# First layer's modulation as columns out of TensorE, and the context's h in two vector passes

## The chip, the cores and the metric

The kernel runs on one core of one Trainium2 chip. The metric is the device time of one execution in microseconds (us). The core has five engines that run side by side, each with its own program: TensorE (PE, with its weight loads shown apart as PEld), VectorE (DVE), ScalarE (ACT), GpSimd (POOL) and SyncE (SP, which issues most DMAs). Each engine works through its program in order and waits on semaphores of the others.

## The reference

Two transformer blocks of two layers each follow one another, all in float32 on 512 latent tokens of 1024 features; the first block has 256 context tokens too. The change touches only what stands ahead of the first layer's projection:

```python
mod = c_silu @ ada_w + ada_b             # (1, 3072): shift, scale, gate
mod_c = cctx_silu @ ada_w + ada_b        # the same weights, the context's vector
shift, scale, gate = jnp.split(mod, 3, axis=-1)
shift_c, scale_c, gate_c = jnp.split(mod_c, 3, axis=-1)
hx = rmsnorm(x, norm_w) * (1 + scale[:, None, :]) + shift[:, None, :]
hc = rmsnorm(cx, norm_w) * (1 + scale_c) + shift_c
px = split_cols(hx @ w_in)
pc = split_cols(hc @ w_in)
```

## The kernel before

Activations lie transposed: features on the 128 partitions (8 tiles `k`), tokens along the free dimension. A float32 product of large matrices is made of three products in `mm3` (L289 to L291): each operand is split into a high part and a low remainder, and hi·hi, hi·lo and lo·hi are summed. For weights ACT makes the high part (`whi<-wraw`, L203) and DVE the remainder (`wlo`, L204); `Weights` does that one tile ahead of its use.

`start` is the stage in question. SP loads x (four DMAs), the vectors, and 16 tiles `aw` of 512 KB: the shift and scale columns of the first layer's modulation weights, cut into four chunks of 512 columns, in the order `ADA0`. `ada0` makes one chunk in 8 matmuls of full float32 (L409): the two condition vectors (`ccol`, 128x2) are the stationary operand, 512 weight columns stream past, and 2 rows of 512 results appear. ACT copies the rows out of PSUM (L412), four transposes on PE turn them into columns (`adac`, L415), and DVE copies these (L416). `mods` (L430, L434) adds the bias and makes the scale columns `acol`. One float32 matmul stands in the trace as two records, a load and a matmul each.

Between them stand the norm of x (squares on ACT, sums on DVE, four matmuls against ones at L249, a power on POOL at L259, four transposes `rrow` at L266 that spread it over the partitions, and eight multiplications of x in place at L583), and the same for the context `cx`, whose loads come last. `h` makes hx in two halves of four tiles, then hc: ACT writes the high part (L589), DVE the full value `hmod` (L590) and the remainder (L591). The first half of hx needs the first two chunks, the second half all four. The first projection tile (`dps<-hx,whi`, L289) follows: 8 tiles k times three matmuls.

A tile framework decides the order of the instructions on each engine when the program is built; the order differs from the code's, and is fixed from then on.

Of the kernel before, what the change touches and what calls it, by code (L numbers as in the profile page):

```python
# [9 lines left out]
F32 = mybir.dt.float32  # L10
# [3 lines left out]
AF = mybir.ActivationFunctionType  # L14
OP = mybir.AluOpType
# [4 lines left out]
D = 1024  # L20
KD = 8
N = 512
NC = 256
# [47 lines left out]
def fr(ap):  # L71
    return ap.bitcast(F32)


class Weights:
# [139 lines left out]
    def next(self, n=None):  # L215
        at = self.n_use
        if self.extra is None:
            self.cut(at + (n or self.depth))
        else:

            self.cut(at + min(n or 2, 2))
            with self.tc.issue_after(self.K.mm_last):
                self.cut(at + (n or self.depth))
                while self.sums and self.sums[0][0] <= at:
                    _, f, m, kc = self.sums.pop(0)
                    f(m, kc)
        self.load(len(self.loads))
        return self.ready.pop(0)[1:]
# [48 lines left out]
def drain(g):  # L277
    for _ in g:
        pass


class Kern:
# [4 lines left out]
    def mm3(self, ps, hi, lo, xh, xl, start, stop):  # L287
        mm = self.nc.tensor.matmul
        mm(ps, hi, xh, start=start, stop=False)  # L289
        mm(ps, hi, xl, start=False, stop=False)  # L290
        self.mm_last = mm(ps, lo, xh, start=False, stop=stop).ins  # L291
        return self.mm_last
# [103 lines left out]
    def ada0(self, part, aw):  # L396


        nc, a, c = self.nc, self.a, self.cst
        if part == 0:  # L400
            self.mod0 = self.adap.tile([128, 24, 2], F32, tag="mod0", bufs=1, name="mod0")
        for ch in ADA0[2 * part:2 * part + 2]:
            ps = self.pt("d", "adaps")
            for g in range(4):
                next(aw, None)
                t = self.aw.pop(0)
                for kk in range(2):
                    k = 2 * g + kk
                    nc.tensor.matmul(ps[0:2, :], self.cc[:, k, :], t[:, kk, :], start=k == 0, stop=k == 7)  # L409
                yield  # L410
            row = self.adap.tile([128, D], F32, tag="adaw", name="adarow")[0:2, :512]
            nc.scalar.activation(row, ps[0:2, :], AF.Copy)  # L412
            pc = self.pt("pt", "adac")
            for t in range(4):
                nc.tensor.transpose(pc[:, 2 * t:2 * t + 2], row[:, t * 128:(t + 1) * 128], self.ident[0:2, 0:2])  # L415
            nc.vector.tensor_copy(self.mod0[:, 4 * ch:4 * ch + 4, :], pc[:, :8].rearrange("p (t s) -> p t s", s=2))  # L416
            yield

    def mods(self, l, cols=((0, 24),)):
# [140 lines left out]
    def start(self, s):  # L560

        nc, a = self.nc, self.a
        V, A = nc.vector, nc.scalar
        self.tmp = s.enter_context(self.tc.tile_pool(name="tmp0", bufs=3))
        xp = s.enter_context(self.tc.tile_pool(name="xp0", bufs=1))
        x = xp.tile([128, 8, N], F32, name="x")
        cx = xp.tile([128, 8, NC], F32, name="cx")
        aw = self.ada0_load(xp)
        for k in range(0, 8, 2):
            nc.sync.dma_start(x[:, k:k + 2, :], a["xt"][:, k:k + 2, :])  # L570
            if k:
                next(aw)
        for _ in range(9):
            next(aw)

        def norm(t, n):
            acc = xp.tile([128, 512], F32, tag="acc", bufs=2, name="acc")
            for k in range(8):
                self.sq_acc(acc[:, :n], t[:, k, :], k)
            nm = Norm(self)  # L580
            nm.part([acc], 0, n)
            for k in range(8):
                V.tensor_tensor(t[:, k, :], t[:, k, :], nm.R[:, :n], op=OP.mult)  # L583

        def h(t, n, hs, s_, k0):
            for k in range(k0, k0 + 4):
                sc, sh = self.A[0][:, k, s_:s_ + 1], self.mod[0][:, k, s_:s_ + 1]
                m = self.tmp.tile([128, 512], F32, tag="hmod", name="hmod")
                A.activation(hs[0][:, k, :], t[:, k, :], AF.Identity, bias=sh, scale=sc)  # L589
                V.tensor_scalar(m[:, :n], t[:, k, :], sc, sh, op0=OP.mult, op1=OP.add)  # L590
                V.tensor_tensor(hs[1][:, k, :], m[:, :n], fr(hs[0][:, k, :]), op=OP.subtract)  # L591

        norm(x, N)
        for i in range(2):
            drain(self.ada0(i, aw))
            self.mods(0, [(4 * i, 4 * i + 4), (8 + 4 * i, 12 + 4 * i)])
            if i:
                with self.tc.issue_after(self.last_load.ins):
                    self.W.load(1)
                    for k in range(0, 8, 4):  # L600
                        nc.sync.dma_start(cx[:, k:k + 4, :], a["ctxt"][:, k:k + 4, :])
                    self.W.load(3)
            h(x, N, self.hx, 0, 4 * i)
        norm(cx, NC)
        for i in range(2):
            h(cx, NC, self.hc, 1, 4 * i)

    def useg(self, i, k, o):

# [742 lines left out]
class Block2:  # L1352
# [155 lines left out]
    def seven(self, pool, banks):  # L1508
# [7 lines left out]
        def product(ps, b, start):  # L1516
            hi, lo = K.W.next()
            for k in range(4):
                mm(ps, hi[:, k, :], b[0][:, k, :], start=k == 0 and start, stop=False, skip_group_check=True)  # L1519
                mm(ps, hi[:, k, :], b[1][:, k, :], start=False, stop=False, skip_group_check=True)  # L1520
                K.mm_last = mm(ps, lo[:, k, :], b[0][:, k, :], start=False, stop=k == 3, skip_group_check=True).ins  # L1521
                self.step()
# [892 lines left out]
```

## Time and profile before

| | |
|---|---|
| median of 3 runs | 2479.59 us (2479.31 to 2483.43) |
| the profiled execution | 2483.87 us |
| its span, first to last instruction | 2482.1 us |
| PE busy | 2354.0 us (95%), 14392 matmul records |
| DVE busy | 1902.7 us (77%) |
| ACT busy | 1326.0 us (53%) |
| mean granted TensorE clock | 0.983 |

The span is the time from the first to the last instruction on the core; what is left of the execution's own time, 1.8 us, lies around it. The granted clock is TensorE's: 1.00 is 2.4 GHz and 0.50 is 1.2 GHz.

### The profile page before, as it was taken

What the parts mean: (1) busy time and instruction counts of PE and PEld (TensorE: products, weight loads), DVE (VectorE), ACT (ScalarE), POOL (GpSimd) and SP (SyncE); (2) the same over time, 40 slices, a digit from 0 to 9 for tenths busy, and PEclk for the clock granted to TensorE, in tenths of its full rate; (3) what the DMA queues carried; (4) which work ended last, traced back from release to release, by engine and by line L of the source; (5) the groups of instructions that cost most, each with busy time, mean ns of one, the idle gap of its engine ahead of it and who ended that gap; (6) DMA issues with size and microseconds to landing.
All of it is one profiled execution on the core that took longest, in us unless ns stands there. A gap on an engine that the chain in (4) does not pass through costs nothing. (4 is left out here: it accounts for less than half of the span.)

```text
span 2482.1 us, 37640 instructions
## 1 busy us (share of the span) xinstructions
PE 2354.0 (95%) x14392; PEld 2028.6 (82%) x14392; DVE 1902.7 (77%) x3337; ACT 1326.0 (53%) x2595; POOL 113.0 (5%) x138
## 2 busy tenths in 40 slices
PE   7899999999999999999998899999999799999998
PEld 3788888888887788888786678989898578899997
DVE  5778777888457888798669868989767985967674
ACT  3566555667345665568644455535354455545453
POOL 0100000000011100000010101000001010100000
PEclk9999999999999999999999999999999999999999
DMA  6112333223422136641432122675432212242422
GB/s 257 51 50 92 96 105 100 85 88 100 153 81 76 45 124 204 211 131 50 135 99 67 58 63 86 215 242 208 141 102 74 69 57 68 85 137 69 136 65 72
DMA packets 87749, 269.67 MB, mean 109 GB/s; under 512 B 12049, under 2 KB 22545, under 8 KB 87185
## 3 DMA queue, kind: packets, MB, share of 16 engines
q1 hardware_dynamic: 78240, 232.79, 29.1%
q10 hardware_dynamic: 6912, 25.17, 2.9%
q0 software_dynamic: 2416, 9.31, 1.0%
q8 instruction: 113, 1.85, 0.3%
q14 instruction: 68, 0.55, 0.1%
HBM read 255.82 MB, written 11.40 MB: 108 GB/s over the span
## 5 line engine op out<-in xcount | busy, mean ns | idle before, releaser
L289 PE MATMUL dps<-hx,whi 128*128 128x512 f32 (+1 forms) x1040 | 412.7, 398 | 22.1 <-ACT q L1744 8.1
L291 PE MATMUL dps<-hx,wlo 128*128 128x512 f32 (+1 forms) x1040 | 400.1, 386 | 8.3 <-DVE wlo L204 4.3
L290 PE MATMUL dps<-hx,whi 128*128 128x512 f32 (+1 forms) x1040 | 401.0, 387 | 5.7 <-DVE hx L523 4.4
L203 ACT ACTIVATE whi<-wraw 128x1024 fp32r<-128x1024 f32 (+2 forms) x202 | 194.1, 964 | 272.6 <-issue 93.6
L204 DVE TENSOR_TENSOR wlo<-wraw,whi 128x1024 fp32r<-128x1024 f32 (+1 forms) x182 | 209.3, 1151 | 75.9 <-ACT whi L203 74.5
L289 PEld LDWEIGHTS dps<-hx,whi 128*128 128x128 f32 x1040 | 200.9, 193 | 51.3 <-ACT q L1744 8.9
L291 PEld LDWEIGHTS dps<-hx,wlo 128*128 128x128 f32 x1040 | 200.2, 193 | 44.5 <-DVE wlo L204 5.2
L290 PEld LDWEIGHTS dps<-hx,whi 128*128 128x128 f32 x1040 | 200.5, 193 | 31.5 <-DVE hx L523 7.1
L1162 ACT ACTIVATE ph<-PT 128x512 fp32r<-128x512 f32 (+1 forms) x280 | 152.8, 559 | 136.1 <-PE PT L1157 132.8
L1163 DVE TENSOR_TENSOR pl<-PT,ph 128x512 fp32r<-128x512 f32 (+1 forms) x280 | 175.2, 641 | 43.4 <-ACT ph L1162 41.2
L161 ACT ACTIVATE whi<-wraw 128x512 fp32r<-128x512 f32 x200 | 118.7, 625 | 102.5 <-PE spt L1520 38.4
L1145 PE MATMUL Y<-ph,vt 128*128 128x256 f32 (+1 forms) x592 | 161.8, 283 | 6.7 <-ACT ph L1162 2.8
L1157 PE MATMUL PT<-ident,P 128*128 128x128 f32 x1024 | 160.5, 276 | 5.8 <-DVE pl L1163 4.0
L1146 PE MATMUL Y<-pl,vt 128*128 128x256 f32 (+1 forms) x592 | 163.1, 291 | 2.4 <-DVE pl L1163 2.2
L290 PE MATMUL w2p<-g,whi 128*128 128x512 f32 (+1 forms) x364 | 140.9, 387 | 1.0 <-DVE g L299 1.0
L289 PE MATMUL w2p<-g,whi 128*128 128x512 f32 (+1 forms) x364 | 140.8, 387 | 0.0
L291 PE MATMUL w2p<-g,wlo 128*128 128x512 f32 (+1 forms) x364 | 140.6, 387 | 0.0
L1157 PEld LDWEIGHTS PT<-ident,P 128*128 128x128 f32 x1024 | 119.0, 141 | 23.1 <-DVE pl L1163 9.8
L1145 PEld LDWEIGHTS Y<-ph,vt 128*128 128x128 f32 x592 | 112.2, 190 | 28.5 <-ACT ph L1162 19.5
L1096 PE MATMUL S<-kt,qt 128*128 128x256 f32 (+2 forms) x576 | 127.3, 329 | 1.6 <-DVE nm L1114 0.9
L1146 PEld LDWEIGHTS Y<-pl,vt 128*128 128x128 f32 x592 | 112.3, 190 | 13.5 <-DVE pl L1163 6.0
L1115 ACT ACTIVATE P<-P,nm 128x512 f32<-128x512 f32 (+1 forms) x128 | 94.9, 742 | 47.7 <-DVE nm L1114 46.1
(474 smaller groups left out, 6387.6 us busy)
## 6 DMA issues: line engine op xcount, KB each, us to landing
wraw<-ffn_w SPq DMA_DIRECT2D x120, 512.0 KB, 4.4
wraw<-w_in SPq DMA_DIRECT2D x112, 512.0 KB, 3.5
adaw<-ada_wt SPq DMA_DIRECT2D x80, 512.0 KB, 4.0
adab<-ada_wt ACTq DMA_DIRECT2D x48, 512.0 KB, 5.1
wraw<-w_out SPq DMA_DIRECT2D x32, 384.0 KB, 3.1
aw<-ada_w SPq DMA_DIRECT2D x16, 512.0 KB, 10.2
wraw<-w_out SPq DMA_DIRECT2D x16, 512.0 KB, 3.5
bias<-bias_b SPq DMA_DIRECT2D x16, 384.0 KB, 3.7
```

Of the source, the lines that this page charges most:

```text
L161: self.nc.scalar.activation(hi[:, j * w:j * w + w], x, AF.Copy)
L203: s = self.nc.scalar.activation(hi[:, q], t[:, q], AF.Copy)
L204: v = E.tensor_tensor(lo[:, q], t[:, q], fr(hi[:, q]), op=OP.subtract)
L289: mm(ps, hi, xh, start=start, stop=False)
L290: mm(ps, hi, xl, start=False, stop=False)
L291: self.mm_last = mm(ps, lo, xh, start=False, stop=stop).ins
L1096: mm(S[:, so:so + n], Q[:, j, qc], Kt[:, i, ko:ko + n], start=i == 0, stop=i == 1)
L1145: mm(o, v, ph[:, co:co + w], start=b == 0 and n == 0, stop=False, skip_group_check=True)
L1146: mm(o, v, pl[:, co:co + w], start=False, stop=b == len(banks) - 1 and n == len(items) - 1, skip_group_check=True)
L1157: nc.tensor.transpose(pst[:, col:col + 128], ps[t][:, pc:pc + 128], K.ident)
L1162: A.activation(ph[:, :col], pst[:, :col], AF.Copy)
L1163: V.tensor_tensor(pl[:, :col], pst[:, :col], fr(ph[:, :col]), op=OP.subtract)
```

## The change

`ada0` swaps the operands. A 128x128 piece of the weights is now the stationary operand and `ccol`, two columns wide, streams past it, so that the results come out as columns; 32 matmuls make a chunk in place of 8, and ACT's copy and the four transposes are gone. For the context, the three passes of DVE (times R in place, scale and shift, remainder) become two: cx times scale times R into `hmod`, then shift and remainder in one. ACT writes hc's high part from `hmod`, so it now comes after DVE's first pass. Line numbers behind the first part of the diff fall by 3 up to `start`, and rise by 3 behind it.

```diff
             for g in range(4):
                 next(aw, None)
-                t = self.aw.pop(0)
+                w = self.aw.pop(0)
                 for kk in range(2):
                     k = 2 * g + kk
-                    nc.tensor.matmul(ps[0:2, :], self.cc[:, k, :], t[:, kk, :], start=k == 0, stop=k == 7)
+                    for t in range(4):
+                        nc.tensor.matmul(ps[:, 2 * t:2 * t + 2], w[:, kk, t * 128:(t + 1) * 128], self.cc[:, k, :],
+                                         start=k + t == 0, stop=k == 7, skip_group_check=True)
                 yield
-            row = self.adap.tile([128, D], F32, tag="adaw", name="adarow")[0:2, :512]
-            nc.scalar.activation(row, ps[0:2, :], AF.Copy)
-            pc = self.pt("pt", "adac")
-            for t in range(4):
-                nc.tensor.transpose(pc[:, 2 * t:2 * t + 2], row[:, t * 128:(t + 1) * 128], self.ident[0:2, 0:2])
-            nc.vector.tensor_copy(self.mod0[:, 4 * ch:4 * ch + 4, :], pc[:, :8].rearrange("p (t s) -> p t s", s=2))
+            nc.vector.tensor_copy(self.mod0[:, 4 * ch:4 * ch + 4, :], ps[:, :8].rearrange("p (t s) -> p t s", s=2))
...
-        norm(cx, NC)
-        for i in range(2):
-            h(cx, NC, self.hc, 1, 4 * i)
+        R = norm(cx, NC)
+        for k in range(8):
+            sc, sh = self.A[0][:, k, 1:2], self.mod[0][:, k, 1:2]
+            m = self.tmp.tile([128, 512], F32, tag="hmod", name="hmod")[:, :NC]
+            V.scalar_tensor_tensor(m, cx[:, k, :], sc, R, op0=OP.mult, op1=OP.mult)
+            A.activation(self.hc[0][:, k, :], m, AF.Identity, bias=sh)
+            V.scalar_tensor_tensor(self.hc[1][:, k, :], m, sh, fr(self.hc[0][:, k, :]), op0=OP.add, op1=OP.subtract)
```

The change also moves the order. On PE, at the start of the program, before (`adaps` is a chunk's result in PSUM, `ssum` and `rrow` the norm of x, `dps` the first projection tile):

```order
L409 MATMUL adaps<-aw,ccol 2x512 x5
L249 MATMUL ssum<-ones,acc 128x1 x4
L409 MATMUL adaps<-aw,ccol 2x512
L266 MATMUL rrow<-ident,rstd 128x128 x4
L409 MATMUL adaps<-aw,ccol 2x512 x3
L415 MATMUL adac<-ident,adarow 128x2 x4
L409 MATMUL adaps<-aw,ccol 2x512 x8
L415 MATMUL adac<-ident,adarow 128x2 x4
L409 MATMUL adaps<-aw,ccol 2x512 x8
L415 MATMUL adac<-ident,adarow 128x2 x4
L409 MATMUL adaps<-aw,ccol 2x512 x7
L289 MATMUL dps<-hx_78,whi 128x512
```

The same place on PE in the changed program, up to the norm of the context:

```order
L410 MATMUL adaps<-ccol,aw 128x2 x24
L249 MATMUL ssum<-ones,acc 128x1 x4
L266 MATMUL rrow<-ident,rstd 128x128 x4
L410 MATMUL adaps<-ccol,aw 128x2 x104
L289 MATMUL dps<-hx_78,whi 128x512
```

Three quarters of the modulation's matmuls now stand behind `rrow`, all of them still ahead of the first projection. The context's norm (`ssum` of two, then `rrow` of two) comes 9 and 11 projection matmuls into the first tile; before, it came 12 and 22 matmuls in.

On ACT, in the same stretch, before (`hx_78` is the high part of hx, `whi` that of a weight tile, `sq` and `acc` the context's squares):

```order
L412 ACTIVATE adarow<-adaps 2x512 x2
L589 ACTIVATE hx_78<-x,mod_228,acol_230 128x512 x4
L412 ACTIVATE adarow<-adaps 2x512
L203 ACTIVATE whi<-wraw 128x1024
L510 ACTIVATE acc<-cx 128x256
L513 ACTIVATE sq<-cx 128x256 x3
L412 ACTIVATE adarow<-adaps 2x512
L513 ACTIVATE sq<-cx 128x256 x4
L203 ACTIVATE whi<-wraw 128x1024
L589 ACTIVATE hx_78<-x,mod_228,acol_230 128x512 x4
```

On ACT in the changed program:

```order
L586 ACTIVATE hx_78<-x,mod_262,acol_264 128x512 x8
L507 ACTIVATE acc<-cx 128x256
L510 ACTIVATE sq<-cx 128x256 x4
L203 ACTIVATE whi<-wraw 128x1024
L510 ACTIVATE sq<-cx 128x256 x3
L203 ACTIVATE whi<-wraw 128x1024
L608 ACTIVATE hc_98<-hmod,mod_262 128x256 x3
```

The first weight tile's high part, which stood ahead of the second half of hx, now stands behind all eight tiles of hx and five passes over the context.

On DVE in the changed program, from the last two chunks' copies (`mod_185`) to the context's `rstd`:

```order
L413 COPY mod_185<-adaps 128x8
L427 SCALAR_TENSOR_TENSOR mod_262<-mod_185,vecs 128x8
L431 SCALAR_TENSOR_TENSOR acol_264<-mod_262,vecs 128x8
...
L587 TENSOR_SCALAR hmod<-x,acol_264,mod_262 128x512
L511 TENSOR_TENSOR acc<-acc,sq 128x256
L588 TENSOR_TENSOR hx_79<-hmod,hx_78 128x512
L511 TENSOR_TENSOR acc<-acc,sq 128x256 x3
L204 TENSOR_TENSOR wlo<-wraw,whi 128x1024
L511 TENSOR_TENSOR acc<-acc,sq 128x256 x2
L204 TENSOR_TENSOR wlo<-wraw,whi 128x1024
L511 TENSOR_TENSOR acc<-acc,sq 128x256
L258 TENSOR_SCALAR rstd<-ssum 128x2
```

The first weight tile's remainder `wlo` and the context's sums, which stood ahead of the fourth chunk's copy or beside it, now stand behind it. From about the 320th of 14273 matmuls on, PE's order is the same in both programs.

## Rows read from the trace of the kernel before

**Rows 1.** The page's first part: busy us, share of the span, instructions.

```profile
PE 2354.0 (95%) x14392; PEld 2028.6 (82%) x14392; DVE 1902.7 (77%) x3337; ACT 1326.0 (53%) x2595; POOL 113.0 (5%) x138
```

**Rows 2.** Busy time by stretch: length, each engine's busy us, then TensorE's clock, DMA.

```profile
9.87:15.00 5.13, 5.13 (x7) 0.77 (x8) 2.12 (x4) 2.21 (x4) 0.00 (x0) 1.00 1.02 413
15.00:43.40 28.40, 28.00 (x83) 6.75 (x81) 13.93 (x30) 6.95 (x13) 1.02 (x1) 1.00 0.95 363
```

**Rows 3.** Timeline, the modulation's matmuls: start us, us, engine, line, count, idle before.

```profile
9.87 7.00 PE L409 MATMUL adaps<-aw,ccol 128*2 128x512 f32 x10 [9.87 <-DMA aw<-ada_w]
...
13.24 0.13 PEld L409 LDWEIGHTS adaps<-aw,ccol 128*2 128x2 f32 x1 [0.73 <-issue]
14.10 0.13 PEld L409 LDWEIGHTS adaps<-aw,ccol 128*2 128x2 f32 x1 [0.73 <-issue]
...
22.79 7.03 PE L409 MATMUL adaps<-aw,ccol 128*2 128x512 f32 x16
```

**Rows 4.** Timeline, the norm of x and the first transposes of a chunk.

```profile
16.80 0.97 PEld L249 LDWEIGHTS ssum<-ones,acc 128*128 128x128 f32 x8 [0.86 <-DVE acc L514]
...
19.20 0.65 PE L266 MATMUL rrow<-ident,rstd 128*128 128x128 f32 x4 [0.40 <-POOL rstd L259]
...
22.45 0.32 PEld L415 LDWEIGHTS adac<-ident,adarow 2*128 2x128 f32 x4 [0.86 <-ACT adarow L412]
```

**Rows 5.** Line L249, loads of 128x128 f32: ns min/median/max, first and last start.

```profile
L249 PEld LDWEIGHTS ssum<-ones,acc x44: 186/192/338, 16.8 to 2472.8; 128*128 128x128 f32 x44
```

**Rows 6.** Timeline of the weight loads near 1873 us, inside a stretch at clock 0.50.

```profile
1873.65 0.54 PEld L249 LDWEIGHTS ssum<-ones,acc 128*128 128x128 f32 x2
1874.07 0.33 PEld L289 LDWEIGHTS dps<-hx,whi 128*128 128x128 f32 x1
```

**Rows 7.** Busy time by stretch near 1260 us, columns as in rows 2.

```profile
1257.50:1260.80 3.30, 3.01 (x26) 3.01 (x27) 0.62 (x4) 1.72 (x4) 0.00 (x0) 1.00 0.04 14
1261.00:1264.20 3.20, 2.70 (x14) 2.41 (x13) 0.75 (x2) 0.87 (x2) 1.07 (x2) 0.50 0.03 5
```

**Rows 8.** The first of these stretches, line L249 alone: PE, PEld, clock, DMA.

```profile
1257.50:1260.80 3.30, 1.67 (x14) 1.73 (x14) 1.00 0.04 14
```

**Rows 9.** Timeline of DVE and ACT: a chunk's copy, half of hx, the first weight.

```profile
30.18 0.17 DVE L416 COPY mod<-adac 128x8 f32<-128x8 f32 x1 [5.14 <-PE adac L415]
...
30.79 2.93 ACT L589 ACTIVATE hx<-x,mod,acol 128x512 fp32r<-128x512 f32 x4 [1.21 <-DVE acol L434]
...
34.62 0.69 DVE L591 TENSOR_TENSOR hx<-hmod,hx 128x512 fp32r<-128x512 f32 x1
...
36.84 1.04 ACT L203 ACTIVATE whi<-wraw 128x1024 fp32r<-128x1024 f32 x1
...
37.91 1.23 DVE L204 TENSOR_TENSOR wlo<-wraw,whi 128x1024 fp32r<-128x1024 f32 x1
38.09 1.01 ACT L513 ACTIVATE sq<-cx 128x256 f32<-128x256 f32 x3
...
39.05 1.48 DVE L514 TENSOR_TENSOR acc<-acc,sq 128x256 f32<-128x256 f32 x3
```

**Rows 10.** Timeline of PE and DVE, first projection tile and the context's norm.

```profile
43.47 0.50 PE L289 MATMUL dps<-hx,whi 128*128 128x512 f32 x1
...
52.06 0.43 PE L266 MATMUL rrow<-ident,rstd 128*128 128x128 f32 x2 [0.67 <-POOL rstd L259]
...
54.36 0.40 PE L289 MATMUL dps<-hx,whi 128*128 128x512 f32 x1
54.60 0.40 PE L290 MATMUL dps<-hx,whi 128*128 128x512 f32 x1
```

**Rows 11.** Timeline of DVE, the first and last of the context's 24 passes.

```profile
52.52 2.74 DVE L583 TENSOR_TENSOR cx<-cx,rrow 128x256 f32<-128x256 f32 x8
...
59.78 0.75 DVE L591 TENSOR_TENSOR hc<-hmod,hc 128x256 fp32r<-128x256 f32 x2
```

**Rows 12.** Groups of DVE by form: busy us, mean ns, idle before.

```profile
L523 DVE SCALAR_TENSOR_TENSOR hc<-hmod,mod,hc 128x256 fp32r<-128x256 f32 x8 | 3.5, 482 | 1.2 <-ACT hc L522 1.2
```

More of the change, by code (lines that the diff above doesn't have):

```diff
@@ L581, in norm, with h @@
             nm.part([acc], 0, n)
-            for k in range(8):
-                V.tensor_tensor(t[:, k, :], t[:, k, :], nm.R[:, :n], op=OP.mult)
-        def h(t, n, hs, s_, k0):
+            return nm.R[:, :n]
+        def h(k0):
+            hs = self.hx
             for k in range(k0, k0 + 4):
-                sc, sh = self.A[0][:, k, s_:s_ + 1], self.mod[0][:, k, s_:s_ + 1]
+                sc, sh = self.A[0][:, k, 0:1], self.mod[0][:, k, 0:1]
                 m = self.tmp.tile([128, 512], F32, tag="hmod", name="hmod")
[L589 to L593, printed above, removed]
+                A.activation(hs[0][:, k, :], x[:, k, :], AF.Identity, bias=sh, scale=sc)
+                V.tensor_scalar(m, x[:, k, :], sc, sh, op0=OP.mult, op1=OP.add)
+                V.tensor_tensor(hs[1][:, k, :], m, fr(hs[0][:, k, :]), op=OP.subtract)
+        R = norm(x, N)
+        for k in range(8):
+            V.tensor_tensor(x[:, k, :], x[:, k, :], R, op=OP.mult)
         for i in range(2):
@@ L602, in start @@
                     self.W.load(3)
-            h(x, N, self.hx, 0, 4 * i)
-        norm(cx, NC)
-        for i in range(2):
-            h(cx, NC, self.hc, 1, 4 * i)
+            h(4 * i)
+        R = norm(cx, NC)
+        for k in range(8):
+            sc, sh = self.A[0][:, k, 1:2], self.mod[0][:, k, 1:2]
[3 more added lines that the diff above has]
+            V.scalar_tensor_tensor(self.hc[1][:, k, :], m, sh, fr(self.hc[0][:, k, :]), op0=OP.add, op1=OP.subtract)
     def useg(self, i, k, o):
```

## The prediction

> **What bounds the kernel now.** The page's first part comes first: PE is busy for 95% of the span [rows 1], so whatever keeps PE from its large matmuls is paid nearly in full. The timeline then shows the stage that the change touches. PE takes up the modulation at 9.87 us, when the first weight tile lands [rows 3], and the first projection matmul stands at 43.47 [rows 10]; in between PE is hardly ever idle, 28.00 of the 28.40 us from 15.0 on [rows 2]. So PE sets the end of this stage, and the weights' arrival only its beginning. Within it two speeds are seen: the loads of the modulation stand 0.86 us apart at 13.24 and 14.10 [rows 3], while sixteen records of a later chunk take 7.03, of which the last lasts some 0.6, so 0.43 each. That is a clock of half and of full speed, although the view by stretch prints 1.00 for both [rows 2]: a clock that has not yet changed shows there as full. PE got its full clock only after some 5 us of 512-column matmuls back to back, near 15 us.
>
> The last 2420 us are not touched: the order on PE is the same there. The forecast is therefore the shift of one point early on, after which PE is again full.
>
> **What the change does to PE's work.** Before: 32 matmuls, 64 records of 0.43, 27.5 us at the full clock. After: 128 matmuls of two columns, 256 records, each with a load of a 128x128 float32 tile. The nearest row is the norm's sum (L249), which has the same load and one column: eight loads in 0.97 us, the last lasting 0.19, so 0.11 apart at the full clock [rows 4, 5]; two loads from 1873.65 to the next at 1874.07, so 0.21 apart, at half clock [rows 6]. A quarter of the 0.86 that 512 columns took at that clock would be 0.215; I reckon with 0.213. Hence 28 us at full clock, as much as before, or 54 at half. The clock decides.
>
> For the clock I take two stretches. It rose near 15 us behind wide matmuls [rows 3]. It fell between 1257.5 and 1264.2: PE was busy for 3.01 of 3.30 us, and so were its loads, yet the next stretch shows 0.50 [rows 7]; 14 of the 26 matmuls there were one-column sums, busy for 1.67 [rows 8]. That PE was busy with loads did not keep the clock up there, and the new chunks are loads and two columns each, with no wide matmul between them. I take half clock from the first to the last of the 256 records.
>
> The page "TensorE: Matmul & The Clock Gate" of the Trainium skill, section LDWEIGHTS, puts a load at its columns over 1.2, which makes 107 ns for 128, with no word of the clock. By it the 256 records would cost 27 us and the kernel would come out within a few us of before. The trace agrees at the full clock (0.11) and not at half (0.21).
>
> **The sum, step by step.**
> 1. 24 matmuls, 48 records of 0.213 from 9.87: to 20.1.
> 2. The sum of x, 8 records: to 21.8. DVE's and POOL's step to `rrow`: before, from 17.77 to 19.20, 1.4 [rows 4], and nothing fills it now: 23.2. Four transposes of 0.21: 24.1.
> 3. 104 matmuls, 208 records: 44.3, to 68.4. PE is done with the modulation 25 us later than before.
> 4. The first projection needs the first weight's high part, and ACT makes that only behind all of hx and five passes over cx. All four chunks must be in before the second half of hx. Copy 0.1 after the last matmul; from copy to first tile of hx 0.6 (30.18 to 30.79); four tiles 2.9; five passes over cx 0.31 apart (three in 1.01, one being 0.4), 1.55; the weight 1.04 [rows 9]; 0.1 to PE. That is 6.3, all of it PE idle, since the projection is next in its program. First projection matmul at 74.7, against 43.47: 31.2 later. Before, that weight was made at 36.84, under the modulation, which was its cover.
> 5. What is late next is `wlo`, behind DVE's half of hx (30.79 to 35.31, 4.5 [rows 9]) and four sums of 0.53 with dependence (three in 1.48): started near 75.3, ready at 76.6, where PE's third matmul would stand at 75.6. One us idle. Projection matmuls stand 0.24 apart at full clock (54.36 to 54.60 [rows 10]), so some 0.45 at half; seven of these, to 79.7; DVE's last sum of the context is there at 79.2, behind the second `wlo`. The context's sum, four records at half clock, to 80.6; DVE, POOL and the latencies before `rrow` as in step 2, 1.4: `rrow` at 82.0. Queued behind it are 13 of the first tile's 24 matmuls; before, at 52.06, there were 2 left [rows 10]. Eleven more at 0.24 are 2.6. So the point where the first tile ends is shifted by 82.0 + 2.6 − 52.06 = 32.5 us; at half clock the eleven cost 5.0, and it is 34.9. I take the clock as up by then, 5 us after wide matmuls began.
> 6. The context's h: 24 passes of DVE took 8.0 us, 52.52 to 60.53 [rows 11]. Sixteen remain, scalar_tensor_tensor of 128x256; 0.48 each alone [rows 12], or 7.7, and 5.5 if they overlapped as the first eight of the old ones did (2.74, 0.34 each). Saved: 0.3 to 2.5 us of DVE. Before, PE had the second tile's matmuls to do meanwhile; after, it has 13 of the first tile and then these, which is longer than the wait for the first tiles of hc, so of the saving I count 0 to 1 us on the path, and take 0.5.
> 7. ACT's copies and PE's transposes vanish: four loads in 0.32 a chunk on PE [rows 4], already in the comparison of end times. Moving ACT's high part of hc behind DVE's first pass costs DVE nothing while three tiles are in flight; uncovered it would be some 0.4 us once.
>
> Shift: 32.5 − 0.5 = 32 us. The rows are of one execution of 2483.87 us (span 2482.1 and 1.8 around it), which lies 4.3 above the median; the shift put on it is 2516, put on the median of 2479.59 it is **2512**, which I give.
>
> **The rivals.**
> *The clock rises all the same* (8 in 100): loads back to back count as work. Then 24 matmuls end at 17.7, `rrow` at 20.5, 208 records of 0.111 end at 43.6, the same as before, and step 4 puts the first projection at 50; with the rest of step 5 at full clock the shift is 6, with a clock fallen in the 6 us wait 8: 2486 to 2488. For it: that the old start rose with the same kind of continuous work; against it rows 7 and 8. The same page, Part 1, says that the throttled state is the default and that sustained matmul activity releases it; whether two columns behind a full load are such activity decides between this rival and the forecast, and the rows speak for the latter.
> *A load costs 0.11 at half clock too* (2): first projection near 47, cold, and a shift of 4: 2484. Against: [rows 6].
> *Faster: the loads hide* (3). Four loads of transposes took 0.32, so 0.06 to 0.08 apart [rows 4]. If the new loads went at 0.06 and the clock rose, the modulation would end at 31.6, the first projection start at 38, and the point of step 5 come 5 us earlier: 2474. It decides from about 0.08 us a record downwards; the sums at L249 show 0.11.
> *The wait behind hx does not bite* (7): the projection starts with the modulation's end and is paced by hx, as before; 25 later plus 2.4 of half clock: 2507.
> *The clock stays down longer behind the wait* (15): past the context's norm, 2514 to 2518.
> The forecast has 65.
>
> A measurement of this kernel can tell 0.2%, 5 us, from no change. The range takes in the forecast, with some 4 us either way for where the clock falls later on and for the runs' own scatter, the wait that does not bite, and most of the longer half clock: 2500 to 2522, leaving out the rest, 18 in 100. Slower by over 0.2%: the forecast, the two variants and most of the first rival, 0.93. Within: 0.05. Faster: 0.02.
>
> **What would show it.** In the new profile: L410's loads 0.21 apart up to the end, near 68; a granted clock that shows its first rise only behind the first `dps` matmuls, near 80; an idle time of about 6 us on PE ahead of L289, ended by ACT's `whi`; `rrow` of the context near 82; and from the second projection tile on, the same waits as before, 32 us later. Loads 0.11 apart from 15 us on make the first rival true. A first projection matmul near 69 takes away step 4. If the shift is there at 100 us and gone at the end, the later stages had room that I don't see in a PE that is busy for 95%.

## The result and the profile after

The changed kernel takes 2508.36 us (median of 5 runs, 2505.78 to 2514.42) against 2479.59 before: ratio 1.0115, 95% interval 1.0098 to 1.0132, or 24 to 33 us more. The forecast was 2512, in a range of 2500 to 2522. The profiled execution of after took 2514.42 us, 30.6 above that of before.

The page's first part, as [rows 1], shows 30 us more of PE and 55 more of its loads, and the same share of the span for PE:

```profile
PE 2383.6 (95%) x14568; PEld 2083.8 (83%) x14568; DVE 1902.4 (76%) x3329; ACT 1321.8 (53%) x2591; POOL 111.9 (4%) x138
```

The timeline of PE from the start of the modulation to the first projection tile, which answers [rows 3, 4, 10] (start us, us, line, count, idle before):

```profile
10.00 10.37 PE L410 MATMUL adaps<-ccol,aw 128*128 128x2 f32 x48 [10.00 <-DMA aw<-ada_w]
20.23 1.84 PE L249 MATMUL ssum<-ones,acc 128*128 128x1 f32 x8
23.43 1.12 PE L266 MATMUL rrow<-ident,rstd 128*128 128x128 f32 x4 [1.35 <-POOL rstd L259]
24.34 44.37 PE L410 MATMUL adaps<-ccol,aw 128*128 128x2 f32 x208
74.85 0.79 PE L289 MATMUL dps<-hx,whi 128*128 128x512 f32 x1 [6.14 <-ACT whi L203]
...
76.59 0.79 PE L291 MATMUL dps<-hx,wlo 128*128 128x512 f32 x1 [0.52 <-DVE wlo L204]
...
81.62 0.69 PE L266 MATMUL rrow<-ident,rstd 128*128 128x128 f32 x2
...
85.52 0.63 PE L290 MATMUL dps<-hx,whi 128*128 128x512 f32 x1
85.94 0.46 PE L291 MATMUL dps<-hx,wlo 128*128 128x512 f32 x1
86.24 0.39 PE L289 MATMUL dps<-hx,whi 128*128 128x512 f32 x1
```

208 records in 44.37 us are 0.213 each. The projection matmuls stand 0.43 apart up to 85.94 and then take 0.39 where they took 0.63: there the clock doubles, for the first time in this execution, 11 us after the first projection matmul. What ACT and DVE did around the wait of 6.14 us answers [rows 9, 11]:

```profile
69.35 2.93 ACT L586 ACTIVATE hx<-x,mod,acol 128x512 fp32r<-128x512 f32 x4 [24.37 <-DVE acol L431]
...
72.49 1.36 ACT L510 ACTIVATE sq<-cx 128x256 f32<-128x256 f32 x4
73.76 1.04 ACT L203 ACTIVATE whi<-wraw 128x1024 fp32r<-128x1024 f32 x1
...
87.14 0.60 ACT L968 ACTIVATE ft<-dps 128x512 f32<-128x512 f32 x1 [2.98 <-PE dps L291]
```

```profile
68.75 0.17 DVE L413 COPY mod<-adaps 128x8 f32<-128x8 f32 x1 [13.29 <-PE adaps L410]
...
82.34 1.27 DVE L607 SCALAR_TENSOR_TENSOR hmod<-cx,acol,rrow 128x256 f32<-128x256 f32 x3 [1.56 <-PE rrow L266]
...
88.17 0.88 DVE L609 SCALAR_TENSOR_TENSOR hc<-hmod,mod,hc 128x256 fp32r<-128x256 f32 x2 [2.20 <-ACT hc L608]
...
90.81 0.48 DVE L609 SCALAR_TENSOR_TENSOR hc<-hmod,mod,hc 128x256 fp32r<-128x256 f32 x1 [0.18 <-ACT hc L608]
```

The view by stretch shows how a full PE hides this. Columns as in [rows 2]:

```profile
24.50:66.00 41.50, 41.50 (x197) 41.50 (x196) 10.37 (x23) 2.93 (x4) 0.00 (x0) 1.00 0.35 132
```

PE and its loads are busy for all of 41.50 us. The clock printed as 1.00 is the one that [rows 2] also print for the first 5 us: no change had been recorded yet. The spacing of the loads tells the clock, the column does not.

### The profile page after: what moved, and what is told of

It is laid out like the page before. It is cut to its first block, busy times and chain, and to the rows that moved or that the text cites. A ratio compares the mean times of both kernels' runs of the same rounds, so it can differ in the third digit from the quotient of the medians.

```text
span 2512.4 us, 37972 instructions
## 1 busy us (share of the span) xinstructions
PE 2383.6 (95%) x14568; PEld 2083.8 (83%) x14568; DVE 1902.4 (76%) x3329; ACT 1321.8 (53%) x2591; POOL 111.9 (4%) x138
## 5 line engine op out<-in xcount | busy, mean ns | idle before, releaser
L290 PEld LDWEIGHTS dps<-hx,whi 128*128 128x128 f32 x1040 | 202.0, 195 | 30.9 <-DVE hx L520 7.4
L1160 PE MATMUL PT<-ident,P 128*128 128x128 f32 x1024 | 159.1, 275 | 5.9 <-DVE pl L1166 4.3
L291 PE MATMUL w2p<-g,wlo 128*128 128x512 f32 (+1 forms) x364 | 140.7, 387 | 0.0
L1160 PEld LDWEIGHTS PT<-ident,P 128*128 128x128 f32 x1024 | 118.6, 140 | 22.8 <-DVE pl L1166 9.8
```

The source lines that it names most:

```text
L1160: nc.tensor.transpose(pst[:, col:col + 128], ps[t][:, pc:pc + 128], K.ident)
```

## The experiments

The theory: the 256 loads are no dearer than the 64 wide records were, and the loss comes from TensorE's clock, which stays at half under loads with two columns each; the rest is order behind it. The rivals: the load itself is dear, the context's new passes cost or save something, or the wait of 6 us is the cause. Ten kernels ran; the table names each by its edit. "Before" is the kernel before, measured beside it on the same chip.

| kernel | median us | before | ratio (95%) |
|---|---|---|---|
| first part alone | 2508.14 | 2477.24 | 1.0130 (1.0116 to 1.0145) |
| second part alone | 2475.92 | 2477.24 | 0.9991 (0.9983 to 1.0000) |
| clock raised ahead of it | 2508.00 | 2477.24 | 1.0124 (1.0109 to 1.0140) |
| wide matmuls between | 2509.81 | 2477.24 | 1.0134 (1.0112 to 1.0156) |
| 128 columns | 2477.26 | 2478.67 | 0.9991 (0.9982 to 1.0000) |
| 32 columns | 2509.62 | 2478.67 | 1.0121 (1.0107 to 1.0136) |
| first weight first | 2508.74 | 2478.67 | 1.0118 (1.0104 to 1.0132) |
| second part, clock raised | 2474.56 | 2478.67 | 0.9981 (0.9972 to 0.9990) |
| 128 columns, clock raised | 2477.71 | 2479.84 | 0.9993 (0.9984 to 1.0001) |
| 64 columns | 2506.15 | 2479.84 | 1.0101 (1.0082 to 1.0120) |

**The two parts apart.** The first kernel takes `ada0` from the changed kernel and the rest from before; the second the reverse:

```diff
-                    nc.tensor.matmul(ps[0:2, :], self.cc[:, k, :], t[:, kk, :], start=k == 0, stop=k == 7)
+                    for t in range(4):
+                        nc.tensor.matmul(ps[:, 2 * t:2 * t + 2], w[:, kk, t * 128:(t + 1) * 128], self.cc[:, k, :],
+                                         start=k + t == 0, stop=k == 7, skip_group_check=True)
```

> The change's first part alone: the modulation with the weights stationary; the context's h keeps its three vector passes. My theory puts all of the loss here: L410's loads 0.213 us apart up to about 68.5 us, the first projection matmul near 75, and a time 26 to 32 us above the kernel before, 2506 to 2512. The rival, that the new order of the context's h (ACT's high part behind DVE's first pass) costs or saves some us of the 28.8, would show as a difference from the changed kernel of more than 2 us; the forecast's own figure for it was 0.5.

> The change's second part alone: the old modulation, and the context's h in two vector passes. My theory: 16 passes of 0.48 in place of 24 that took 8.0 us, with ACT between the two of a tile; between 1.5 us saved and 1 us lost, so 2478 to 2481, no change that can be told. Rival: the second part saves a visible 3 us or more by itself (to 2476 or below) and the first part costs more than the whole change shows; or it costs 3 us or more because the first pass waits for ACT.

All of the loss is in the first part (30.9 us). The second part alone is 1.3 us lower than before, with an interval that just touches no change; that is the size expected, the kernel before being 2.4 us lower in this set of runs. Its first and last passes on DVE, with the short waits for ACT's high part:

```profile
52.14 1.26 DVE L610 SCALAR_TENSOR_TENSOR hmod<-cx,acol,rrow 128x256 f32<-128x256 f32 x3
53.63 1.28 DVE L612 SCALAR_TENSOR_TENSOR hc<-hmod,mod,hc 128x256 fp32r<-128x256 f32 x3 [0.23 <-ACT hc L611]
...
58.25 0.88 DVE L612 SCALAR_TENSOR_TENSOR hc<-hmod,mod,hc 128x256 fp32r<-128x256 f32 x2 [0.19 <-ACT hc L611]
```

16 passes take 52.14 to 59.13, 7.0 us against 8.0 in [rows 11]. In the changed kernel the same passes take 82.34 to 91.29, 9.0 us, because ACT is held at `ft`, which waits for the first projection tile: 2.20 us of DVE, ahead of L609 in the rows of after.

**The clock raised ahead of the modulation, and wide matmuls between.**

```diff
         aw = self.ada0_load(xp)
+        wp = self.pt("y", "warm")
+        for _ in range(26):
+            nc.tensor.matmul(wp, self.wide[:, :128], self.wide, start=True, stop=True)
```

The second kernel has these too, and the same wide matmul behind each narrow one in `ada0`.

> The changed kernel with 26 matmuls of 512 columns (bf16, 128x128 stationary, into a spare PSUM tile that nothing uses) at the start of the program, ahead of the modulation, while the first weights are still on their way. They bring TensorE's clock up before the modulation begins. My theory is that loads with two columns each do not keep it up: the clock falls soon after they take over, the loads go from about 0.11 us apart to 0.21, and the time is 0 to 4 us below the changed kernel, 2504 to 2508. Rival: the clock only has to be raised once and steady loads hold it; then the loads stay 0.11 us apart to the end, the modulation ends near 44 us in place of 68.5, and the time is 20 to 25 us lower, 2483 to 2488.

> The kernel of warm_after, and besides one matmul of 512 columns (bf16, result used by nothing) behind each of the modulation's 128 matmuls of two columns. This adds some 28 us of PE's work at full clock. My theory, that it is the half clock and not the load itself that makes the modulation long: the wide matmuls hold the clock up, L410's two loads with the wide one take about 0.45 us, and the modulation ends at 68 to 74 us, at or little behind the changed kernel's 68.5 although PE has twice the work; L410's loads that follow on each other are about 0.11 us apart. Rival: a float32 load of 128x128 with a narrow matmul behind it costs 0.21 us at either clock; then a step takes some 0.65 us and the modulation ends near 95. In this program's order ACT makes the first weight ahead of the second half of hx, so the idle 6 us ahead of the first projection should be gone as well.

With the clock raised first, the timeline of the loads and the view by stretch show it fall again (columns as in [rows 2]):

```profile
9.21 1.92 PEld L412 LDWEIGHTS adaps<-ccol,aw 128*128 128x128 f32 x16 [0.16 <-issue]
11.93 6.04 PEld L412 LDWEIGHTS adaps<-ccol,aw 128*128 128x128 f32 x32 [0.80 <-DMA aw<-ada_w]
```

```profile
9.20:12.40 3.20, 2.49 (x22) 2.39 (x21) 1.70 (x4) 1.15 (x2) 0.00 (x0) 1.00 1.03 399
13.00:18.00 5.00, 5.00 (x25) 5.00 (x25) 1.39 (x2) 1.15 (x2) 0.00 (x0) 0.50 1.03 419
22.00:66.00 44.00, 44.00 (x209) 44.00 (x208) 10.37 (x23) 2.93 (x4) 0.00 (x0) 0.50 0.37 147
```

The first 16 loads stand 0.115 apart, the next 32 on average 0.18, those from 22 us on 0.21, and now the column prints 0.50 over the same 0.21 that it called 1.00 in the changed kernel. Raising the clock once gained nothing that the time shows. PE also waited for weights there, 0.7 us ahead of the load at 11.93, but such waits do not explain the fall: the two kernels with the same start under "Faster than both" waited as long (0.67 twice; 0.88 and 0.50), and their clock stayed at 1.00. The framework put about half of the wide matmuls of the other kernel into groups, all of them before 50 us, and from there on one behind each pair of records:

```profile
65.77 0.28 PE L412 MATMUL adaps<-ccol,aw 128*128 128x2 f32 x2
65.91 0.38 PE L414 MATMUL warm<-wide 128*128 128x512 bf16 x1
66.12 0.28 PE L412 MATMUL adaps<-ccol,aw 128*128 128x2 f32 x2
...
68.41 0.58 PE L289 MATMUL dps<-hx,whi 128*128 128x512 f32 x1
```

```profile
24.50:34.00 9.50, 9.50 (x41) 7.88 (x40) 5.12 (x10) 0.00 (x0) 0.00 (x0) 0.50 0.97 348
43.00:68.40 25.40, 25.04 (x209) 22.99 (x213) 6.39 (x14) 5.10 (x9) 0.00 (x0) 1.00 0.20 63
```

In the steady stretch two narrow records and a wide matmul take 0.35 us (65.77 to 66.12) at clock 1.00; in the changed kernel two narrow records alone take 0.43. I had expected about 0.45 for the three. In the first of the two windows, where the narrow records stand in groups of sixteen, the clock is at 0.50. The first projection stands at 68.41, earlier than in the changed kernel, with 128 wide matmuls more in front of it. So it is the clock, and not the load, that makes the modulation long; the time is still that of the changed kernel, since the wide matmuls are work too.

**More columns behind each load.** The two condition columns are repeated; here for 128:

```diff
-                        nc.tensor.matmul(ps[:, 2 * t:2 * t + 2], w[:, kk, t * 128:(t + 1) * 128], self.cc[:, k, :],
+                        nc.tensor.matmul(ps[:, 128 * t:128 * t + 128], w[:, kk, t * 128:(t + 1) * 128],
+                                         self.cc[:, k, None, :].to_broadcast([128, 64, 2]),
```

> The changed kernel with a wider moving operand: the two condition columns are repeated 64 times, so that 128 columns stream past each load and 126 of the results are used by nothing. By the trace of before 512 columns took 0.43 us a record at full clock, so 128 take 0.107, about what the load takes, and the loads ran beside the streaming in the kernel with wide matmuls between. My theory: the same 256 loads no longer cost 0.21 because the clock rises within some 10 us of the start; the records then stand 0.11 to 0.12 us apart, the modulation ends at 41 to 46 us in place of 68.5, and the time is 2480 to 2489, 20 to 28 below the changed kernel. Rival one, the loads keep the clock down whatever streams between them: 0.21 apart as before, 2505 to 2512. Rival two, load and columns add up and the clock rises: 0.22 apart at full clock, an end near 68, and 2505 to 2512 with the granted clock showing 1.00; the clock and the spacing tell the two apart.

> The same with 32 columns (the two repeated 16 times). 32 columns take 0.027 us at full clock and 0.053 at half, by the quarter and the sixteenth of what 512 took. My theory expects the clock to stay at half to the modulation's end, loads 0.21 apart and a time within 4 us of the changed kernel, 2504 to 2512, since PE still spends most of each record on the load alone. Rival: a few more columns are enough, and the modulation ends near 45 with a time of 2482 to 2489.

> The changed kernel with 64 moving columns (62 results used by nothing): between 32, at which the clock stayed at half, and 128, at which it rose. The load covers the streaming at either clock, so only the clock can make a difference: at half, records 0.21 apart and 2504 to 2511; at full, 0.11 apart and 2475 to 2482. My theory does not say which; I put a little more on half, since PE would still be on loads alone for half of each record. A spacing between the two with a clock that goes up and down is the third case.

The modulation's matmuls with 128 columns, then with 32, then with 64 (timeline of PE):

```profile
9.39 6.81 PE L410 MATMUL adaps<-ccol,aw 128*128 128x128 f32 x36 [9.39 <-DMA aw<-ada_w]
...
18.83 24.28 PE L410 MATMUL adaps<-ccol,aw 128*128 128x128 f32 x216
42.87 0.48 PE L289 MATMUL dps<-hx,whi 128*128 128x512 f32 x1
```

```profile
23.44 44.42 PE L410 MATMUL adaps<-ccol,aw 128*128 128x32 f32 x208
74.00 0.79 PE L289 MATMUL dps<-hx,whi 128*128 128x512 f32 x1 [6.14 <-ACT whi L203]
```

```profile
22.40 44.47 PE L410 MATMUL adaps<-ccol,aw 128*128 128x64 f32 x208
66.64 0.77 PE L289 MATMUL dps<-hx,whi 128*128 128x512 f32 x1
...
70.16 0.79 PE L291 MATMUL dps<-hx,wlo 128*128 128x512 f32 x1 [2.33 <-DVE wlo L204]
```

With 128 columns 216 records take 24.28 us, 0.112 each, and the time is that of the kernel before: 32.4 us below 32 columns on the same chip, with the same 256 loads. With 32 and 64 they stay 0.21 apart to the end. For 32 the expectation held; for 64 I had named no winner. For 128 the spacing and the end at 43 held, and the time came out below my 2480 to 2489. The order moves as well: with 64 and 128 columns, unlike with 32, ACT makes the first weight ahead of the second half of hx, and the wait of 6.14 us is gone. With 64 the kernel takes 2506 us all the same, so neither that order nor the wait is what 128 columns win. The two windows of the 128-column kernel place the rise of the clock: 24 records in 5.10 us, then 212 in 23.50.

```profile
9.40:14.50 5.10, 5.10 (x24) 5.10 (x25) 2.52 (x5) 2.15 (x4) 0.00 (x0) 1.00 1.02 403
19.00:42.50 23.50, 23.50 (x212) 23.50 (x212) 13.11 (x28) 7.93 (x14) 0.00 (x0) 1.00 0.98 378
```

**The first weight ahead of the second half of hx.** The first tile is cut first, and `h` is ordered behind it:

```diff
-            h(4 * i)
+                self.W.cut(1)
+            if i:
+                first, rest = self.W.last
+                with self.tc.issue_after(first), self.tc.issue_after(rest):
+                    h(4 * i)
+            else:
+                h(4 * i)
```

> The changed kernel, with the first weight tile cut ahead of the second half of hx, as it stood before the change; the modulation's matmuls are the changed kernel's. My theory: the 6.1 us idle time of PE ahead of the first projection matmul is the wait behind hx and goes; the first projection stands near 69 in place of 74.85. What is late next is the context's norm, whose sums on DVE still stand behind the second half of hx: in the kernel with wide matmuls between, which has this order, PE waited 1.6 and 1.0 us there and the context's rrow came at 78.9 against 81.6. So 2 to 4 us of the 6 reach the end: 2504 to 2507. Rival: the wait costs nothing in the end, since the clock's rise and the context's norm are what the tile ends on: within 1 us of the changed kernel. Second rival: all 6 us are won, 2502 or below.

```profile
68.63 0.77 PE L289 MATMUL dps<-hx,whi 128*128 128x512 f32 x1
...
77.37 0.40 PE L291 MATMUL dps<-hx,wlo 128*128 128x512 f32 x1
80.28 0.60 PE L249 MATMUL ssum<-ones,acc 128*128 128x1 f32 x4 [2.51 <-DVE acc L511]
81.92 0.69 PE L266 MATMUL rrow<-ident,rstd 128*128 128x128 f32 x2 [1.03 <-POOL rstd L259]
```

```profile
81.40:88.20 6.80, 6.02 (x21) 5.14 (x22) 5.55 (x14) 2.93 (x7) 0.46 (x1) 0.50 0.00 0
```

The idle time ahead of the first projection is gone, and 2508.74 us shows no gain. PE is through the first tile's 24 matmuls at 77.8, 9 us before the changed kernel, and then waits 2.51 and 1.03 us for the context's norm; `rrow` comes at 81.92 against 81.62, and behind these waits the clock is at 0.50 from 81.4 to 88.2. So the norm and the clock take back what the wait gave: the changed kernel is through the first 277 records of PE behind its modulation at 127.8 us, this one at 129.1. Later it is 1.7 us ahead (268.88 against 270.55 for the same matmul), but the changed kernel has a half-clock stretch of its own in between, from 140.7 on. My 2 to 4 us did not come, and the first rival is right by the medians; their intervals (0.14% either way) leave room for 2 or 3 us.

**Faster than both.** The clock raised at the start, with the old modulation and the context's two passes, and with 128 columns:

> The old modulation (512 columns stream past), the context's h in two passes, and 26 matmuls of 512 columns (bf16, result used by nothing) at the start of the program, before the first weights land. They bring the clock up before 9.84 us, and the wide modulation keeps it up: its first 5 us at half clock cost some 2.6 us, which are won as far as the weights' arrival allows it. Theory: 2473 to 2475, 1 to 3 us below the second part alone. Rival: the weights' arrival takes over as the bound, or the clock falls in a wait for it, and nothing is won.

> The kernel with 128 moving columns (126 results used by nothing), with the 26 matmuls of 512 columns (used by nothing) at the start of the program. The modulation then begins at full clock, as the wide one did in the fastest kernel so far, and 128 columns keep it up. Theory: the records stand 0.112 us apart from the first, the first projection matmul comes 1 to 2.5 us earlier than 42.87, and the time is 2474 to 2477, 0 to 3 us below 128 columns alone and level with the old modulation warmed the same way. Rival: the arrival of the weights, which the warmed kernel waited for twice (0.67 each), sets the pace, the clock falls in these waits, and nothing is won or some us are lost.

```profile
9.36 1.88 PE L411 MATMUL adaps<-aw,ccol 128*2 128x512 f32 x4 [0.16 <-DMA aw<-ada_w]
11.91 1.88 PE L411 MATMUL adaps<-aw,ccol 128*2 128x512 f32 x4 [0.67 <-DMA aw<-ada_w]
...
42.10 0.50 PE L289 MATMUL dps<-hx,whi 128*128 128x512 f32 x1
```

The first is the fastest kernel here: 0.9981 of before, 4.1 us, with an interval that excludes no change. Its wide records stand 0.43 apart from the first on, and only 1.0 us of the 2.6 that I expected reaches the first projection (42.10 against 43.08 without), because PE now waits for the weights. Against the kernel before it is 1.4 us there (43.47); where the rest of the 4.1 us comes from, no run here separates. With 128 columns the first projection came at 43.17, later than 42.87 unwarmed, so nothing was won, as the rival had it. The clock did not fall in the waits, though: 216 of the 256 records stand behind `rrow` of x, which waits for POOL, and start at 19.14 here and at 18.83 unwarmed:

```profile
9.85 2.02 PE L412 MATMUL adaps<-ccol,aw 128*128 128x128 f32 x16
12.74 2.05 PE L412 MATMUL adaps<-ccol,aw 128*128 128x128 f32 x16 [0.88 <-DMA aw<-ada_w]
15.30 0.71 PE L412 MATMUL adaps<-ccol,aw 128*128 128x128 f32 x4 [0.50 <-DMA aw<-ada_w]
...
18.65 0.65 PE L266 MATMUL rrow<-ident,rstd 128*128 128x128 f32 x4 [0.80 <-POOL rstd L259]
19.14 24.28 PE L412 MATMUL adaps<-ccol,aw 128*128 128x128 f32 x216
```

## Why the prediction was right, step by step

| step | predicted | in the trace of after |
|---|---|---|
| 1, 24 matmuls | to 20.1 | 20.23 |
| 2, `rrow` of x and its transposes | 23.2 to 24.1 | 23.43 to 24.34 |
| 3, 208 records | to 68.4 | 68.71 |
| 4, idle, first projection | 6.3, at 74.7 | 6.14, at 74.85 |
| 5, `wlo`, `rrow` of the context | 76.6, 82.0 | 76.59, 81.62 |
| 5, shift where the first tile ends | 32.5 (34.9 at half clock) | 34.1 (`tps`, 53.65 to 87.80) |
| 6, the context's two passes on DVE | 0.3 to 2.5 saved | 1.0 longer |
| shift of the end | 32 | 30.6 by the profiles, 28.8 by the medians |

**The mechanism** is shown. 128 columns in place of two, the loads unchanged, bring back the time of before; 32 and 64 do not. That also settles the first three rivals: the clock did not rise under the loads, and the loads cost 0.21 at half clock and 0.112 at full, neither 0.11 at half nor 0.06. The Trainium skill, page "TensorE: Matmul & The Clock Gate", section LDWEIGHTS, gives 107 ns for 128 columns without a word of the clock; the trace agrees at full clock alone.

**The wait behind hx** (step 4) has the size and the place that the step gave it, so the rival in which it does not bite is refuted by the trace, though its 2507 lies nearer to the measured median than my 2512. But that rival would sell its removal for 5 us, and removing it gave nothing that the medians show. In the changed kernel PE is busy from 76.59 to the end of the first tile and does not wait for the context's norm, so the 6 us stand in its chain. Without them PE waits for that norm, whose sums stand on DVE behind the second half of hx. `rrow` came at 81.62 with the wait and at 81.92 without it; step 5, which followed both chains, came out right.

**The clock's second rise** was taken too early. I let it be up at `rrow`, 82; it came by 86.24, and the shift was 34.1, near the other bound. That is the condition of the rival in which the clock stays down past the context's norm (15 in 100); its 2514 to 2518 did not come, because of what follows.

**The last 2420 us** were not untouched, and this is the sentence of the prediction that failed. In the traces PE's order is the same in both kernels only from 100.39 us of before (127.81 of after) on; up to there the matmuls over hx and hc are mixed differently. At that point the shift is 27.4, no longer 34.1. From the end of the first tile to a transposition of P just behind it (L1157, now L1160), before took 51.13 us and after 44.08. First before, with the half-clock part of it, then after, columns as in [rows 2]:

```profile
53.65:104.78 51.13, 44.70 (x254) 37.29 (x254) 35.74 (x78) 22.66 (x45) 10.87 (x11) 0.93 0.23 71
96.90:103.80 6.90, 6.50 (x23) 5.41 (x24) 4.95 (x10) 2.13 (x5) 1.64 (x1) 0.51 0.02 6
```

```profile
87.80:131.88 44.08, 39.66 (x247) 34.27 (x247) 31.89 (x65) 21.31 (x42) 10.71 (x11) 1.00 0.24 70
```

Idle time fell from 6.4 to 4.4 us; six matmuls over hc (0.7 us) were done ahead of this part in after; and the half-clock stretch from 96.90 on, 6.50 us of busy time that I estimate at 3.2 less at full clock, is not in this part of after. The shift is 27.1 at its end, and later waits and clocks bring it to 30.6. How much of this belongs to the change is open: the first such dip begins at 96.9 us in before and at 140.7 in after, and the second part alone, which has the old modulation, shows none up to 806 us. So the forecast came near the measured time in part by luck: the end of the first tile lay 1.6 us behind my 32.5, the stretch up to the common order took 6.7 off, and the rest put 3.2 on. The 28.8 of the medians has an interval of 24 to 33, so it does not tell my 32 from it; the first part alone measured 30.9.

**Step 6** missed its sign on DVE in the changed kernel and had it right alone. On the time no run shows it: with it the ratio is 1.0115, without it (the first part alone) 1.0130, and the intervals overlap. What I left out was `ft`: ACT stands at it until the first projection tile is done, and hc's high parts, which now gate DVE's second pass, stand behind it.

## What to carry to other kernels

When a stationary operand serves only two columns, TensorE spends its time on loads, and the clock can stay at half under loads that fill the engine to 100%: read the spacing of equal records, not the busy share nor a clock column that has seen no change yet. With 128 columns the streaming fitted beside the loads and cost nothing, so a wider moving operand, even of repeated columns, can be the cheapest cure. Before removing an idle time, look for what ends next at the same place; here the norm behind it, and a clock that fell behind the wait for it, took back the 6 us.

## What the runs showed of the hardware

- A 128x128 float32 load ran beside the streaming of the matmul ahead of it. 128 columns behind each load took 0.112 us a record, about what two took at full clock (0.115); behind a matmul of 512 bf16 columns (0.21) the next load was hidden, and the pair of narrow records added 0.14.
- With 2, 32 and 64 columns the clock did not rise in 57 us without a gap of more than 1.4 us on PE; with 128 it rose some 5 us after the first record. The Trainium skill, same page, Part 1, says that the throttled state is the default and that activity releases it; here PE and its loads, busy for 41.50 of 41.50 us, did not release it.
- The same skill's page "Perfetto Trace Analysis", section Identifying the Most-Contended Engine, takes the share of the peak arithmetic and the busy share of the loads, not the busy share of the matmuls, as measures of headroom. Here both busy shares were 100% at half clock and again at full (23.50 of 23.50 us with 128 columns): neither share shows the factor of two.
